# Float16 parts in the output product behind attention, and another order at attention's end

## The chip, the cores and the metric

One Trainium2 chip; the kernel runs on one NeuronCore of it. A core has five engines with a queue each: TensorE (PE, matrix products into PSUM; its weight loads, PEld, run beside it), VectorE (DVE), ScalarE (ACT), GpSimd (POOL) and SyncE (SP). SP and POOL issue most of the DMAs between HBM and SBUF. An engine works its queue in order and waits where an instruction's inputs or buffers are not ready. The metric is the device time of one execution in microseconds (us).

## The reference

A two-layer transformer block on 256 tokens of width 2048, with 256 context tokens beside them. Each layer normalises, shifts and scales its input by vectors made from the condition `c`, runs a mixer of width 4096 and multiplies the mixer's output by `w_out`, gated. Layer 0's mixer is a Fourier branch, for tokens and context. Layer 1's is attention: 64 query heads of size 64 share 8 key and value heads; a token sees a window of tokens and the whole context, with one sink per head. Cut to what matters here:

```python
q, k, v, z = split(h @ w_in)                 # layer 1
kc, vc = split(hc @ w_in[:, kv columns])
o = softmax([q k^T, sink]) v                 # keys: the window and the context
y = o * silu(z)                              # 256 x 4096
x = x + gate * (y @ w_out[1])                # 4096 x 2048: the product that is changed
return rmsnorm(x, final_g)
```

All inputs and the result are float32.

## The kernel before, in words

**Precision.** TensorE takes a product in parts: each operand is split into a high part and a remainder, and three matmuls (high x high, high x low, low x high) are summed in PSUM. `mm3` (lines 144 to 147) issues these three. There are two kinds of parts. With fp32r parts, `split` (lines 65 to 67) casts on ACT and subtracts on DVE, and nothing is scaled. With float16 parts, `split16` (lines 134 to 139) first multiplies by a power of two `up`, so that the parts fit float16's range; the result is scaled back where it leaves PSUM. The power of two comes from the sum of the squares of the whole tensor, so every weight that is to be split this way has to be read and squared once ahead of time.

**Layer 0's output product** (32 steps, lines 1031 to 1075) uses float16 parts in 28 of 32 contraction steps of each half. Beside it run: the squares of layer 1's key and value weights (`scan_loads1`, lines 812 to 822: POOL loads half a tile of 512 KB as two loads, `scan_sums` squares them on ACT, line 827), the adaptive vectors of layer 1 (line 792 on DVE, loads on SP and POOL; its `wa` buffers and the weight parts `wf` share the six buffers of the tag `ws`), and the squares of layer 0's output.

**The layer boundary** (lines 1078 to 1112) sums squares for the norm, turns the result x1 to rows and stores it to `x1d`.

**Keys and values** (lines 1137 to 1227). All 512 rows are split into float16 parts (`hz`, lines 1152 to 1156, on DVE and ACT), 16 contraction steps of 24 matmuls each against `wkv`, whose parts `split16` makes per half tile. In the same stage `make_hx1` (lines 1167 to 1173) builds the fp32r parts of the 256 tokens for the queries and gates.

**Attention** (lines 1234 to 1503). The work is laid out by hand as a list of filler units (`units`, queries, gates and, at the end, the first column block of the output product: 12 units `"o"` of two contraction steps each, 0 to 23) and 66 turns of a loop. Turn `i` emits the scores and the softmax of head `i` (`stage_s`), a filler unit, the product with the values of head `i - 2` (`stage_o`), and another unit. The weights of a head are cast to float16 parts `f` (ACT, DVE; lines 1439 and 1440) and transposed to `ft` by a DMA on SP (line 1442); the last two heads, 62 and 63, are instead transposed by TensorE and evacuated by ACT and DVE (`stage_t`, lines 1445 to 1450). `emit_y` multiplies head outputs with their gates into `y1`, two blocks of 128 channels per tile.

**The product behind attention** (lines 1506 to 1644). `y_split` (lines 1243 to 1249) makes fp32r parts of y: blocks 0 to 15 in the `h1` pool, 16 to 23 in `act` tiles, 24 to 31 in `ys` tiles of the last pool; the subtraction is GpSimd's up to block 23. The 2048 output columns are taken in three passes: `wo1a` (512 columns, in the units, the last four pairs of steps after attention), `wo1b` (1024 columns, 16 tiles of two steps) and `wo1c` (512 columns, 8 tiles of four steps). The weights are split by `half_split`, fp32r. `evac` multiplies by the gate `gbc`, adds x1 (read back from `x1d` into `x2`, eight POOL loads at the start) and squares for the last norm; `finish` scales and stores.

**Order.** The framework plans the order of each engine's queue when the program is built: a list by priority (program order) with a simulated time. `tc.issue_after(ins)` puts what is in its block behind `ins` on that instruction's engine; it is an order, not a wait.

Of the kernel before, what the change touches and what calls it, by code (L numbers as in the profile page):

```python
# [10 lines left out]
F32 = mybir.dt.float32  # L11
# [21 lines left out]
def tile_dit(ctx: ExitStack, tc: tile.TileContext, a: dict, out: bass.AP):  # L33
# [778 lines left out]
    scans1 = iter(range(16))  # L812

    def scan_loads1(n):
        for j in [next(scans1) for _ in range(n)]:
            for q in range(2):
                t = act()
                c = (j % 2 * 2 + q) * 512
                nc.gpsimd.dma_start(t, a["wkv"][j // 2][:, c : c + 512])
                c = j * 2 + q  # L820
                c += 80 if c < 28 else -28
                pend.append((t, scn[:, c : c + 1]))
# [34 lines left out]
    with tc.tile_pool(name="yp", reuse_waits="tile", bufs=32) as ypool:  # L857
# [142 lines left out]
        ada_rate = {**{i: 2 for i in (*range(6, 10), *range(17, 26))}, **{i: 0 for i in (14, 15, 16, 28, 29, 30, 31)}}  # L1000
        hbd = dram.tile([P, 2], F32, name="hbd")
# [26 lines left out]
        for i in range(32):  # L1028
# [9 lines left out]
            scan_loads1({14: 1, 15: 2, 16: 1, 26: 2, 27: 1}.get(i, 1) if 14 <= i < 28 else 0)  # L1038
# [38 lines left out]

    x1d = dram.tile([2, P, D], F32, name="x1d")
# [57 lines left out]
    with tc.tile_pool(name="h1", reuse_waits="tile", bufs=16) as h1p:  # L1136
# [4 lines left out]
        with tc.tile_pool(name="kvp", reuse_waits="tile", bufs=2) as kvp:  # L1141
# [24 lines left out]

            def make_hx1(k):
                hx = h1p.tile([P, 512], F32R, tag="h1", name="h1")
                t = kvp.tile([P, 512], F32, tag="ht", name="ht")[:, 0:N]
                V.scalar_tensor_tensor(t, x1[k][:, 0:N], gs1[:, k, 0:1], r_bc1[:, 0:N], op0=ALU.mult, op1=ALU.mult)  # L1170
                S.activation(hx[:, 0:N], t, AF.Identity, bias=sh1[:, k, 0:1])
                V.scalar_tensor_tensor(hx[:, N : 2 * N], t, sh1[:, k, 0:1], hx[:, 0:N].bitcast(F32), op0=ALU.add, op1=ALU.subtract)
                hx1.append(hx)

            o = [[psum() for _ in range(2)] for _ in range(4)]
            for kg in range(8):
                with tc.issue_after(ends[max(kg * 2 - 1, 0)][0] if kg else sq_end[0]), tc.issue_after(ends[max(kg * 2 - 1, 0)][1]):
                    if kg:
                        wr = raw(a["wkv"][kg])
                    w = [split16(wr, i, upk) if kg or i else w0 for i in range(2)]  # L1180
# [25 lines left out]

            l1 = psum()
# [23 lines left out]
        with tc.tile_pool(name="at", reuse_waits="tile", bufs=2) as at:  # L1231
# [11 lines left out]
            def y_split(k):  # L1243
                if 16 <= k < 24:
                    t = act(F32R)
                else:
                    t = (h1p if k < 16 else fin[0]).tile([P, 512], F32R, tag="h1" if k < 16 else "ys", name="ys", bufs=16)
                split(t[:, 0:N], t[:, N : 2 * N], y1[k // 2][:, (k % 2) * N : (k % 2 + 1) * N], GP if k < 24 else V)
                yh.append(t)

            def o1_step(k, os_, wh, wl):
                while len(yh) <= min(k + 4, NB - 1) and (len(yh) < 24 or fin):
                    y_split(len(yh))
# [60 lines left out]
            def units():  # L1314
# [15 lines left out]
                for k in range(12):  # L1330
                    yield "o", k, 0, None
# [69 lines left out]
            def emit_y(blk):  # L1401
# [5 lines left out]
                V.scalar_tensor_tensor(y1[blk // 2][:, (blk % 2) * N : (blk % 2 + 1) * N], obs[blk, 1], dsc[:, blk // 4 : blk // 4 + 1], szs.pop(blk), op0=ALU.mult, op1=ALU.mult)  # L1407

            def stage_s(i):
# [23 lines left out]
                for tb in range(2):  # L1433
                    if i < 62:
# [4 lines left out]
                    S.activation(f[:, 0:512], pt[tb], AF.Copy, scale=sm[:, tb : tb + 1])  # L1439
                    V.scalar_tensor_tensor(f[:, 512:1024], pt[tb], sm[:, tb : tb + 1], f[:, 0:512], op0=ALU.mult, op1=ALU.subtract)  # L1440
                    if i < 62:
# [47 lines left out]
            for i in range(66):  # L1489
# [3 lines left out]
                if i == 62:  # L1493
                    t = actp.tile([P, 1024], F16, tag="act", name="ident16")
                    ident16.append(t[:, 0:P])
                    S.copy(ident16[0], ident)
                if i < 64:
                    pts[i] = stage_s(i)
                if i - 2 >= 62:
# [7 lines left out]
        with tc.tile_pool(name="fin", reuse_waits="tile", bufs=1) as fp:  # L1507
# [3 lines left out]
            x2 = []  # L1511
            for tb in range(2):
                x2.append([act() for _ in range(4)])
                for c in range(4):
                    nc.gpsimd.dma_start(x2[tb][c], x1d[tb, :, c * 512 : (c + 1) * 512])
            fg = fp.tile([P, D], F32, name="fg")
# [16 lines left out]
            for k in range(24, NB, 2):  # L1533
                w = w1_next()
                for i in range(2):
                    o1_step(k + i, oA, *(t[:, i * 512 : (i + 1) * 512] for t in w))
            for tb in range(2):
                evac(tb, 0, oA[tb])
            o = [[psum() for _ in range(2)] for _ in range(2)]
            for kg in range(16):  # L1540
                w = ws_split(raw(a["wo1b"][kg]))
                for j in range(2):
                    k = kg * 2 + j
                    wh, wl = w[j]
                    for tb in range(2):
                        for c in range(2):
                            q = slice(c * 512, (c + 1) * 512)
                            mm3(o[tb][c], yh[k][:, tb * P : (tb + 1) * P], yh[k][:, N + tb * P : N + (tb + 1) * P], wh[:, q], wl[:, q], k == 0, k == NB - 1)
# [5 lines left out]
            def step(k, tb, wh, wl, q=slice(0, 512), first=0, last=NB - 1):  # L1554
                mm3(o[tb][:, q], yh[k][:, tb * P : (tb + 1) * P], yh[k][:, N + tb * P : N + (tb + 1) * P], wh[:, q], wl[:, q], k == first, k == last)
# [31 lines left out]
            for kg in range(8):  # L1587
                t = raw(a["wo1c"][kg])
                if kg < 5:
                    w = [(h[:, q], l[:, q]) for h, l in ws_split(t) for q in (slice(0, 512), slice(512, 1024))]  # L1590
                else:
                    w = []
                    for i in range(2):
                        if kg * 2 + i < 13:
                            for j in range(2):
                                h, l = act(F32R), act(F32R)
                                split(h, l, t[:, (i * 2 + j) * 512 : (i * 2 + j + 1) * 512])
                                w.append((h, l))
                        else:
                            h, l = half_split(t, i)  # L1600
# [121 lines left out]
```

## Time and profile before

| | |
|---|---|
| median of three runs | 1771.17 us (1769.23 to 1772.79) |
| profiled execution | 1773.51 us |
| its span, first to last instruction | 1771.7 us |
| granted TensorE clock, mean | 0.997 |
| HBM read | 400.43 MB |

How the stages lie in the profiled span, by the first and last instruction on their tiles:

| us | stage |
|---|---|
| 322 to 658 | layer 0's gates (float16 parts) |
| 658 to 998 | layer 0's output product |
| 998 to 1008 | layer boundary |
| 1008 to 1091 | keys and values |
| 1091 to 1618 | queries, gates, attention; first units of the last product from 1570 |
| 1618 to 1762 | the rest of the product behind attention |
| 1762 to 1772 | last norm and stores |

How to read the profile's rows. A group has its line, engine and operation, `out<-in` by the program's names, shapes and types, the count, then busy us in total and mean ns of one, then the idle time of the engine just before it and what ended that. A row of the timeline has the start, the length in us, engine, line, operation and names; in square brackets stands the idle time before it and who ended it. Matmuls overlap, so their lengths exceed the distance of their starts. A DMA group has the issuing queue, the count, the size of one and the median us from issue to landing.

### The profile page before, as it was taken

The numbers are of one execution on the slowest core, as the hardware profiler recorded it, in microseconds if no ns is written. First come the engines' busy times: TensorE is split into PE (matmuls) and PEld (weight loads), VectorE is DVE, ScalarE is ACT, GpSimd is POOL, SyncE is SP. The second block draws the span as 40 slices with busy tenths as digits, with TensorE's granted clock in tenths as the row PEclk, the third lists the DMA queues.
The fourth block names the chain that finished last, engine by engine and source line by source line (L and its number), as shares of the span: only waits on it lengthen the run. The fifth ranks groups of instructions, "written<-read, shape, count | busy, mean of one in ns | idle before, by whom it ended". The sixth has DMA issues, their size and how long they took to land. (4 is left out here: it accounts for less than half of the span.)

```text
span 1771.7 us, 26606 instructions
## 1 busy us (share of the span) xinstructions
PE 1733.6 (98%) x9517; PEld 1188.4 (67%) x9517; DVE 1405.9 (79%) x2454; ACT 1089.2 (61%) x2069; POOL 333.8 (19%) x440
## 2 busy tenths in 40 slices
PE   6999999999999999999999999999999999999997
PEld 4679999544444444446434745788888888887886
DVE  5778889697777786886688695899999999997455
ACT  5545556477777755464324454688888878886343
POOL 0002111212222114121201001412303230234010
PEclk9999999999999999999999999999999999999999
DMA  9998999778988869985976532688987898888544
GB/s 393 418 355 242 288 273 255 288 285 318 330 306 318 313 222 374 364 293 201 367 270 210 170 130 72 190 198 205 216 214 204 216 221 195 206 211 270 190 166 143
DMA packets 229077, 447.29 MB, mean 252 GB/s; under 512 B 155888, under 2 KB 156288, under 8 KB 202064
## 3 DMA queue, kind: packets, MB, share of 16 engines
q1 hardware_dynamic: 182784, 331.93, 58.0%
q0 software_dynamic: 42016, 106.70, 19.4%
q10 hardware_dynamic: 4144, 6.95, 1.2%
q8 instruction: 75, 1.23, 0.3%
q14 instruction: 58, 0.48, 0.1%
HBM read 400.43 MB, written 12.59 MB: 233 GB/s over the span
## 5 line engine op out<-in xcount | busy, mean ns | idle before, releaser
L67 DVE TENSOR_TENSOR wl<-raw,wh 128x1024 fp32r<-128x1024 f32 x197 | 262.6, 1338 | 111.1 <-ACT wh L66 83.0
L66 ACT CAST wh<-raw 128x1024 fp32r<-128x1024 f32 x197 | 205.5, 1045 | 145.5 <-PE ps L146 103.2
L146 PE MATMUL ps<-act,wf 128*128 128x512 f16 x512 | 194.2, 379 | 0.0
L147 PE MATMUL ps<-act,wf 128*128 128x512 f16 x512 | 191.3, 379 | 0.0
L145 PE MATMUL ps<-act,wf 128*128 128x512 f16 x512 | 189.9, 379 | 0.6 <-ACT wf L137 0.3
L1386 PE MATMUL ps<-h,wh 128*128 128x512 f32 x512 | 185.9, 399 | 0.0
L147 PEld LDWEIGHTS <-wf 128*128 128x128 f16 x960 | 93.9, 98 | 118.1 <-DVE wf L138 4.5
L145 PE MATMUL ps<-y,wf 128*128 128x512 f16 x448 | 170.6, 381 | 0.8 <-ACT wf L137 0.8
L147 PE MATMUL ps<-y,wf 128*128 128x512 f16 x448 | 167.3, 381 | 4.0 <-DVE wf L138 4.0
L146 PE MATMUL ps<-y,wf 128*128 128x512 f16 x448 | 170.7, 381 | 0.0
L145 PEld LDWEIGHTS <-wf 128*128 128x128 f16 x960 | 93.8, 98 | 113.6 <-ACT wf L137 4.2
L146 PEld LDWEIGHTS <-wf 128*128 128x128 f16 x960 | 94.0, 98 | 109.5 <-issue 0.8
L137 ACT ACTIVATE wf<-raw,nrm 128x1024 f16<-128x1024 f32 x56 | 63.2, 1145 | 137.8 <-PE ps L147 82.1
L1388 PE MATMUL ps<-h,wl 128*128 128x256 f32 x512 | 139.2, 282 | 0.0
L138 DVE SCALAR_TENSOR_TENSOR wf<-raw,tn,wf 128x1024 f16<-128x1024 f32 x64 | 79.8, 1282 | 42.5 <-ACT wf L137 42.4
L1440 DVE SCALAR_TENSOR_TENSOR f<-p,sm,f 128x512 f16<-128x512 f32 x128 | 104.6, 837 | 8.6 <-ACT f L1439 8.4
L1427 ACT ACTIVATE p<-ps,mx 128x512 f32<-128x512 f32 x128 | 87.8, 688 | 36.7 <-DVE mx L1424 31.8
L790 POOL DMA_DIRECT2D wa<-in_adw x64 | 34.0, 532 | 404.7 <-DVE acc L792 163.5
L1386 PEld LDWEIGHTS ps<-h,wh 128*128 128x128 f32 x512 | 96.9, 189 | 19.1
L1439 ACT ACTIVATE f<-p,sm 128x512 f16<-128x512 f32 x128 | 87.7, 717 | 30.8 <-DMA ft<-f 12.4
L146 PE MATMUL ps<-wl,h 128*128 128x512 f32 x256 | 101.3, 396 | 0.0
L827 ACT ACTIVATE act<-act 128x512 f32<-128x512 f32 x160 | 98.4, 616 | 4.7 <-DMA act<-in_wo 4.4
(414 smaller groups left out, 4676.4 us busy)
## 6 DMA issues: line engine op xcount, KB each, us to landing
raw<-in_wz SPq DMA_DIRECT2D x64, 1024.0 KB, 5.6
raw<-in_awp SPq DMA_DIRECT2D x32, 1024.0 KB, 12.7
zr<-in_adw SPq DMA_DIRECT2D x64, 512.0 KB, 6.9
wa<-in_adw POOLq DMA_DIRECT2D x64, 512.0 KB, 6.3
act<-in_wo POOLq DMA_DIRECT2D x128, 256.0 KB, 7.8
raw<-in_wo SPq DMA_DIRECT2D x32, 1024.0 KB, 8.0
raw<-in_wq SPq DMA_DIRECT2D x32, 1024.0 KB, 5.2
raw<-in_wu SPq DMA_DIRECT2D x32, 1016.0 KB, 6.3
```

The lines of the kernel that those rows point to most:

```text
L66: last_cast[0] = S.copy(h, src).ins
L67: last_sub[0] = eng.tensor_tensor(l, src, h.bitcast(F32), op=ALU.subtract).ins
L138: last_sub[0] = V.scalar_tensor_tensor(w[:, 1], src, up, w[:, 0], op0=ALU.mult, op1=ALU.subtract).ins
L145: PE.matmul(o, wh, xh, start=start, stop=False)
L146: PE.matmul(o, wh, xl, start=False, stop=False)
L147: return PE.matmul(o, wl, xh, start=False, stop=stop).ins
L827: S.activation(t, t, AF.Square, accum_out=c)
L1386: PE.matmul(o[0], wh[:, q], hx1[k], start=k == 0, stop=k == KT - 1)
L1388: PE.matmul(o[0][:, 0:N], wl[:, q], hx1[k][:, 0:N], start=False, stop=False)
L1427: S.activation(pt[tb], so[tb], AF.Exp, bias=mx[:, tb : tb + 1], scale=-1.0, accum_out=sm[:, tb : tb + 1])
L1439: S.activation(f[:, 0:512], pt[tb], AF.Copy, scale=sm[:, tb : tb + 1])
L1440: V.scalar_tensor_tensor(f[:, 512:1024], pt[tb], sm[:, tb : tb + 1], f[:, 0:512], op0=ALU.mult, op1=ALU.subtract)
```

## The change

The product behind attention takes float16 parts for contraction steps 0 to 27 in `wo1b` and `wo1c`; `wo1a`, which is worked on during attention, keeps fp32r parts, and so do steps 28 to 31.

- *Scales.* The sum of the squares of those weights (14 tiles of `wo1b` and 7 of `wo1c`, 42 half tiles) is added to the stream that squared the 16 half tiles of `wkv`. Seven of them are loaded in layer 0's product, with other counts per step (`w_rate`), and 35 in the keys' and values' stage (`loads2`, through four 512 KB buffers `pz`, on POOL), squared there by ACT or, one in three from the fourth weight tile on, by DVE (`sums2`). The squares of y are taken on ACT in attention (`y_sums`, one per tile of two blocks), and `out_scale` makes the powers of two at head 62.
- *Parts.* `y_half` makes float16 parts of y, two blocks at a time, in the `h1` pool, once attention's last cast has been issued, one tile per step. `split16` splits the weights. The weights of steps 28 to 31 are scaled too (`w_scaled`), and the gates' columns 512 and up are scaled back by `dn1`.
- *End of attention.* Head 61 is transposed by TensorE as 62 and 63 are. The list gets 14 units `"o"` (steps 0 to 27) instead of 12. All fp32r parts of y up to block 27 lie in the `h1` pool.
- *Order behind it.* The last two pairs of steps of `wo1a` and its evacuation (`first_rest`) come after the first two tiles of `wo1b`. Of the eight loads of `x2`, two stay at the start, and two each follow at tiles 3, 5 and 7.

```diff
-    scans1 = iter(range(16))
+    yq = adab[:, 1, 0].rearrange("p k s -> p (k s)")
+    wst = [a["wkv"][i] for i in range(8)] + [a["wo1b"][i] for i in range(14)] + [a["wo1c"][i] for i in range(7)]
+    scans1 = iter(range(58))
...
+        w_rate = {10: 1, 11: 1, 14: 2, 15: 2, 16: 2, 17: 1, 18: 1, 20: 1, 22: 1, 24: 1, 26: 2, 27: 2, 28: 3, 29: 2, 30: 1}
...
-            scan_loads1({14: 1, 15: 2, 16: 1, 26: 2, 27: 1}.get(i, 1) if 14 <= i < 28 else 0)
+            scan_loads1(w_rate.get(i, 0))
...
+    V.tensor_reduce(yq[:, 16:17], scn[:, 4:18], axis=AX.X, op=ALU.add)
...
+            def sums2(act_only):
+                for n in range(len(pend)):
+                    t, c = pend.pop(0)
+                    if n < 2 or act_only:
+                        S.activation(t, t, AF.Square, accum_out=c)
+                    else:
+                        V.tensor_tensor_reduce(t, t, t, 1.0, 0.0, ALU.mult, ALU.add, c)
+
+            def loads2(n):
+                for j in [next(scans1) for _ in range(n)]:
+                    t = kvp.tile([P, 1024], F32, tag="pz", name="pz", bufs=4)
+                    nc.gpsimd.dma_start(t, wst[j // 2][:, j % 2 * 1024 : j % 2 * 1024 + 1024])
+                    pend.append((t, scn[:, j - 23 : j - 22]))
...
-                    w = [split16(wr, i, upk) if kg or i else w0 for i in range(2)]
+                    w = []
+                    for i in range(2):
+                        w.append(split16(wr, i, upk) if kg or i else w0)
+                        with tc.issue_after(last_cast[0]), tc.issue_after(ends[min(kg * 4 + i * 2 + 1, 15)][0]):
+                            if kg * 2 + i < 12:
+                                sums2(kg < 3)
+                        with tc.issue_after(pow_end[0]):
+                            loads2((4, 3, 3, 3, 3, 3, 3, 3, 3, 3, 3, 1, 0, 0, 0, 0)[kg * 2 + i])
...
+            sums2(True)
+            V.tensor_reduce(yq[:, 17:18], scn, axis=AX.X, op=ALU.add)
...
-                if 16 <= k < 24:
-                    t = act(F32R)
-                else:
-                    t = (h1p if k < 16 else fin[0]).tile([P, 512], F32R, tag="h1" if k < 16 else "ys", name="ys", bufs=16)
+                t = (h1p if k < 28 else fin[0]).tile([P, 512], F32R, tag="h1" if k < 28 else "ys", name="ys", bufs=16 if k < 28 else 4)
...
+            def y_sums(n, i):
+                while ynext[0] < min(n, len(ypairs)) and ypairs[ynext[0]] <= i - 2:
+                    j = ynext[0]
+                    ynext[0] += 1
+                    S.activation(act(), y1[j], AF.Square, accum_out=yq[:, j : j + 1])
+
+            def out_scale():
+                V.tensor_reduce(yq[:, 18:19], yq[:, 0:14], axis=AX.X, op=ALU.add)
+                o = psum()
+                for c, i, st in ((0, 16, True), (0, 17, False), (1, 18, True)):
+                    PE.matmul(o[:, c : c + 1], ones.broadcast_to([P, P]), yq[:, i : i + 1], start=st, stop=i > 16)
...
+            def y_half(j):
+                t = h1p.tile([P, 1024], F16, tag="h1", name="yf", bufs=16)
+                S.activation(t[:, 0:512], y1[j], AF.Copy, scale=uy)
+                V.scalar_tensor_tensor(t[:, 512:1024], y1[j], uy, t[:, 0:512], op0=ALU.mult, op1=ALU.subtract)
+                for i in range(2):
+                    yf[j * 2 + i] = t[:, i * N : i * N + N], t[:, 512 + i * N : 512 + i * N + N]
...
+            def w_scaled(t, i):
+                h, l = (wsp.tile([P, 1024], F32R, tag="ws", name=n_) for n_ in ("wh", "wl"))
...
-                for k in range(12):
+                for k in range(14):
                     yield "o", k, 0, None
...
-                    if i < 62:
+                    if i < 61:
                         nc.sync.dma_start_transpose(ft[:, :, tb, :], f)
...
+                y_sums(14, i if i < 60 else 99)
+                if i == 62:
+                    out_scale()
...
-                if i - 2 >= 62:
+                if i - 2 >= 61:
                     stage_t(*pts[i - 2])
...
-            for k in range(24, NB, 2):
-                w = w1_next()
-                for i in range(2):
-                    o1_step(k + i, oA, *(t[:, i * 512 : (i + 1) * 512] for t in w))
-            for tb in range(2):
-                evac(tb, 0, oA[tb])
+            with tc.issue_after(f_last[0]), tc.issue_after(f_last[1]):
+                for j in range(3):
+                    y_half(j)
+
+            def first_rest():
+                for k in range(28, NB, 2):
+                    w = w1_next()
+                    for i in range(2):
+                        o1_step(k + i, oA, *(t[:, i * 512 : (i + 1) * 512] for t in w))
+                S.activation(gbc[:, 512:], gbc[:, 512:], AF.Copy, scale=dn1)
+                for tb in range(2):
+                    evac(tb, 0, oA[tb])
...
-                w = ws_split(raw(a["wo1b"][kg]))
+                if kg == 2:
+                    first_rest()
+                t = raw(a["wo1b"][kg])
+                with tc.issue_after(f_last[0]), tc.issue_after(f_last[1]):
+                    w = [split16(t, i, uw) if kg < 14 else w_scaled(t, i) for i in range(2)]
+                if kg + 3 < 14:
+                    with tc.issue_after(last_cast[0]), tc.issue_after(last_sub[0]):
+                        y_half(kg + 3)
+                if kg in (3, 5, 7):
+                    x2_load(kg // 2)
...
-                    w = [(h[:, q], l[:, q]) for h, l in ws_split(t) for q in (slice(0, 512), slice(512, 1024))]
+                    w = [(h[:, q], l[:, q]) for h, l in (split16(t, i, uw) for i in range(2)) for q in (slice(0, 512), slice(512, 1024))]
```

51 lines of the change are left out of this document (36 added, 15 removed).

## The prediction

> **What bounds the kernel now.** I read the page's busy times first, then the waits of TensorE, then a table by stretch, then the matmuls in order of time.
>
> ```profile
> span 1771.7 us, 26606 instructions
> PE 1733.6 (98%) x9517; PEld 1188.4 (67%) x9517; DVE 1405.9 (79%) x2454; ACT 1089.2 (61%) x2069; POOL 333.8 (19%) x440
> ```
>
> TensorE is busy 98% of the span: the time is the sum of its steps plus some 38 us in which it stands still.
>
> ```profile
> PE ps L145 <- DVE dh L254: 12.6, 2, 11.3
> PE ps L1457 <- DMA ft<-f: 4.4, 5, 2.1
> PE ps L147 <- DVE wf L138: 4.0, 1, 4.0
> ```
>
> (Total us, times, longest.) The first is the opening, which the change does not touch. The others lie where it works: five waits for transposes by DMA in attention, and one stall in layer 0's output product.
>
> ```profile
> 660.00:960.00 300.00, 295.18 (x1356) 141.07 (x1354) 232.42 (x358) 136.51 (x255) 66.09 (x124) 0.99 0.83 304
> 1008.00:1088.00 80.00, 80.00 (x373) 36.25 (x371) 60.09 (x116) 40.48 (x71) 0.00 (x0) 1.00 0.39 134
> 1160.00:1560.00 400.00, 399.00 (x2206) 332.83 (x2206) 375.10 (x698) 327.57 (x643) 85.35 (x60) 1.00 0.86 210
> 1590.00:1618.00 28.00, 25.70 (x151) 20.43 (x150) 23.08 (x45) 22.75 (x48) 14.01 (x18) 1.00 0.90 266
> 1628.00:1750.00 122.00, 122.00 (x528) 98.88 (x527) 67.92 (x62) 51.69 (x61) 11.83 (x6) 1.00 0.52 181
> ```
>
> A row has the stretch, its length, the busy time of PE, PEld, DVE, ACT and POOL, the granted clock, the DMA share and GB/s. The rows are layer 0's output product, the keys' and values' projection, attention, its end, and the product behind it. In the second and the last TensorE never stops: there only fewer or quicker matmuls shorten the time, and work added to ACT, DVE or DMA is free until TensorE waits for it.
>
> **The change part by part.** *Matmuls on float16 parts.* Durations overlap, so a matmul's price is the distance between starts. First layer 0's float16 product, then two stretches of the product that changes:
>
> ```profile
> 759.81 0.38 PE L145 MATMUL ps<-y,wf 128*128 128x512 f16 x1
> ...
> 767.58 0.38 PE L145 MATMUL ps<-y,wf 128*128 128x512 f16 x1
> ```
> ```profile
> 1640.00 1.10 PE L145 MATMUL ps<-wh,ys 128*128 128x512 f32 x4
> ...
> 1656.80 1.10 PE L145 MATMUL ps<-wh,ys 128*128 128x512 f32 x4
> ```
> ```profile
> 1676.32 1.07 PE L145 MATMUL ps<-wh,act 128*128 128x512 f32 x4
> ...
> 1689.92 1.07 PE L145 MATMUL ps<-wh,act 128*128 128x512 f32 x4
> ```
>
> Float16: 36 starts in 7.77 us, 215.8 ns. fp32r with y in ys tiles: six steps of 12 matmuls, 72 starts in 16.80 us, 233.3 ns. fp32r with y in act tiles (steps 16 to 23): 60 in 13.60 us, 226.7 ns. Of 32 steps 28 change, 20 of ys and 8 of act, each with 12 matmuls over wo1b and 6 over wo1c. That is 360 x 17.5 ns = 6.3 us and 144 x 10.9 ns = 1.6 us: **-7.9 us**, all of it on the path if the splits keep up.
>
> The Trainium skill (TensorE: Matmul & The Clock Gate, "Weight-path perf modes") says that the array takes one element per cell and cycle whatever its width; for 512 columns the page's start-to-start is 215.7 ns. By that fp32r would run at the same pace, and this term would be 0 instead of -7.9. The float16 rows agree to 0.1 ns; the fp32r rows are 17.6 ns off and decide.
>
> *The splits of that product.*
>
> ```profile
> L137 ACT ACTIVATE wf<-raw,adab 128x1024 f16<-128x1024 f32 x16 | 18.0, 1140 | 11.4 <-PE ps L146 4.4 <-PE ps L147 3.9 <-issue 2.4
> L138 DVE SCALAR_TENSOR_TENSOR wf<-raw,adab,wf 128x1024 f16<-128x1024 f32 x16 | 20.3, 1282 | 4.6 <-ACT wf L137 4.6
> L1439 ACT ACTIVATE f<-p,sm 128x512 f16<-128x512 f32 x128 | 87.7, 717 | 30.8 <-DMA ft<-f 12.4 <-issue 12.1 <-ACT th L1394 5.1
> L1440 DVE SCALAR_TENSOR_TENSOR f<-p,sm,f 128x512 f16<-128x512 f32 x128 | 104.6, 837 | 8.6 <-ACT f L1439 8.4
> ```
>
> A weight tile needs two halves and one y_half: ACT 2 x 1.14 + 0.72 = 3.0 us, DVE 2 x 1.28 + 0.84 = 3.4 us, against 24 x 215.8 ns = 5.2 us of matmuls. Covered, with 1.8 us to spare per tile. Scaling gbc, the three pairs of x2 loads moved down POOL's queue, and the last fp32r steps set behind two tiles have tens of us until their readers; on SP two wo1b tiles go ahead of the last wo1a tile, into three raw buffers as before. Taken at nothing; a cover that fails here costs at most one landing of a tile, some 5 us.
>
> *The end of attention.* Head 61 loses its two DMA transposes on SP and is turned by TensorE; 14 units of the first product instead of 12 fill the last slots, with four more y splits.
>
> ```profile
> 1600.80 0.27 PE L1457 MATMUL ps<-ft,v 128*128 128x256 f16 x1 [1.35 <-DMA ft<-f]
> ...
> 1601.67 0.83 PE L1449 MATMUL ps<-ident,f 128*128 128x128 f16 x12
> ...
> 1612.10 0.28 PE L1457 MATMUL ps<-ft,v 128*128 128x256 f16 x1 [0.94 <-DVE ft L1450]
> ```
>
> The first stall is head 61's: 1.35 us go. The second lies where slots were empty; 24 matmuls now stand there: up to 0.94 us go. 16 more transposes at 0.83 / 12 = 0.07 us are +1.1. out_scale puts three one-column matmuls into TensorE's queue, behind a VectorE sum of squares that are ready by head 60: +0.2 by the same row; the units queued behind them on TensorE would wait with them, if the squares were late. Two more evacuations on busy ACT and DVE, and y_half 0 to 2 with the first split between head 63's last cast and the product's first matmul: ACT 3 x 0.72 + 1.14, DVE 3 x 0.84 + 1.28, some 4 us while 24 to 30 matmuls of 0.23 us, 6 to 7 us, are still queued. What is late next is head 62's own evacuation. I take -0.5; bounds -2.3 (the stalls go, the rest hides) and +4 (nothing of those 4 us hides).
>
> *Squares of y*: 14 on ACT in attention. An existing square with its accumulator read follows its neighbour at 0.61 us:
>
> ```profile
> 894.70 0.61 ACT L827 ACTIVATE act<-act 128x512 f32<-128x512 f32 x1
> ...
> 895.31 0.61 ACT L827 ACTIVATE act<-act 128x512 f32<-128x512 f32 x1
> ```
>
> 14 x 0.61 = 8.6 us, against 400 - 327.6 = 72 us of idle ACT in the attention row. They queue ahead of exponentials and casts, but every head has two turns of slack. +0.5, bounds 0 and +4.
>
> *Squares of the output weights in layer 0's product*: 7 more half tiles, 14 loads and 14 squares, 8.6 us of an ACT that idles 163 of 300 us, and 3.7 MB.
>
> ```profile
> 921.49 1.23 DVE L792 CUSTOM_DVE_ANT_0 wa<-wa,cb 128x1024 f32<-128x1024 f32 x1 [3.27 <-DMA wa<-in_adw]
> ```
> ```profile
> 920.00:925.00 5.00, 1.02 (x4) 0.46 (x5) 3.51 (x6) 2.24 (x5) 0.00 (x0) 0.95 0.77 306
> 925.00:930.00 5.00, 5.00 (x18) 1.92 (x17) 5.00 (x10) 1.18 (x3) 0.53 (x1) 0.71 0.54 169
> ```
>
> The 4 us stall is this ring: VectorE waits for a wa load, the ws buffer it holds keeps ACT from the next wf split, TensorE runs dry, and the clock comes back at 0.71 for 5 us, another 1.5. The Trainium skill (the same page, Part 1) has the clock halve after an idle window of some 3.4 us; this gap was longer than that, and the trace agrees. The new rates thin the loads of these steps (5 half tiles in steps 17 to 25 instead of 9), but the surplus must land somewhere in this stage. 0, bounds -6 (the stall goes) and +6 (a second one).
>
> *Squares in the keys' and values' stage.* 35 half tiles of 512 KB through four pz buffers, loads on POOL, which is idle there.
>
> ```profile
> L645 ACT ACTIVATE pz<-pz 128x1024 f32<-128x1024 f32 x12 | 12.7, 1062 | 2.6 <-DMA pz<-in_wz 2.6
> ```
> ```profile
> wa<-in_adw POOLq DMA_DIRECT2D x64, 512.0 KB, 6.3
> ```
> ```profile
> act<-in_wkv POOLq DMA_DIRECT2D x32, 256.0 KB, 11.3
> ```
> ```profile
> 1039.32 1.15 ACT L137 ACTIVATE wf<-raw,adab 128x1024 f16<-128x1024 f32 x1
> ```
>
> 29 squares go to ACT: 40.5 + 29 x 1.06 = 71 of 80 us. 6 go to DVE, at some 1.3 us each: 60.1 + 8 = 68. Both fit, barely. The danger is the ring: a buffer takes issue, landing and square, about 0.5 + 6.3 + 1.1 = 7.9 us, so a load every 2.0 us, and the 31 behind the first four take 61 us. The steps that hold them last 11 x 24 x 215.8 ns = 57 us. 4 us late, ACT's split behind a square with it; but the split for step 11 was made at 1039, and its matmuls start 57 us after 1008: 26 us ahead. So nothing is lost until the landing passes about 9 us; from there each further us costs 31 / 4 = 7.8. The hz and hx1 casts, on the same queue, come later too. I take +1.5, nearer the row of the same 512 KB than the 256 KB one; bounds 0 and, at 11.3 us, +18.
>
> Sum: -7.9 - 0.5 + 0.5 + 0 + 1.5 = **-6.4 us**. The profiled execution took 1773.5 (span 1771.7 and 1.8 around it), so 1767.1; it lies 2.3 above the median of the runs shown, 1771.17, which gives **1765**.
>
> **The rivals.** *Two stalls go*: the ring at 920 clears with the thinner loads, -5.5 more: 1759 to 1757. For it: the loads leave just those steps; against it: the doubled wa traffic stays. *The ring of pz buffers binds*: the slower one. Demand in this stage is 8 tiles of 1 MB and 35 of 0.5, 26 MB in 80 us, 330 GB/s, more than the 304 of layer 0's row, whose 256 KB loads took 11.3 us. If the landing passes 9 us ACT's queue stands behind squares, TensorE waits for splits, and the clock falls as at 925. At 11.3 us: 1765 + 17 = 1782; slower from 10.3 us on. Against it: queue orders are planned, and squares seldom waited before. *No quicker pace*: fp32r and float16 alike here, only the side costs left, 1771.2 + 1.5 = 1773. Against it: the rows above. *Many small costs*: the upper ends at attention's end, its squares and the 920 ring, each about half, eat the gain: 1768 to 1775.
>
> **How the numbers follow.** Forecast 0.58, with a range of its own of 1760 to 1767.6; two stalls 0.12; pz ring 0.12; no quicker pace 0.05; small costs 0.13. A measurement tells 0.2% from nothing, 3.5 us: faster is below 1767.6, slower above 1774.7. Faster 0.58 + 0.12 = 0.70; same 0.05 + 0.11 = 0.16; slower 0.12 + 0.02 = 0.14. The range 1756 to 1774 leaves out the ring and a little at either end.
>
> **What would show it.** Right: starts at 215.8 ns over wo1b and wo1c, and a stretch from the product's first to its last matmul about 8 us shorter; no wait for transposes by DMA at head 61; TensorE full between the keys' first and last matmul, and that stage still 83 us. Wrong: waits of TensorE for splits there, with ACT waiting for pz loads; a second stall beside 920; TensorE idle between head 63 and the first float16 matmul.

## The result, and the profile after

| | before | after |
|---|---|---|
| median | 1771.46 us (12 runs, 1766.05 to 1774.63) | 1771.95 us (12 runs, 1770.11 to 1774.54) |
| profiled execution, its span | 1773.51, 1771.7 us | 1770.58, 1768.8 us |
| HBM read | 400.43 MB | 422.45 MB |

The recorded ratio to the kernel before, which is not simply the quotient of the two medians, is 0.9998, with a 95% interval of 0.9988 to 1.0009: no change that can be told from none. The time lies in the range of 1756 to 1774, but the forecast of 1765 was 7 us too low, and the most likely outcome, faster, did not come. That the time still lies in the range is luck: without a gain of 2.8 us in layer 0 that the prediction had taken at nothing (e2 below), it would be 1774.8.

The page's busy times after the change:

```profile
span 1768.8 us, 26913 instructions
PE 1728.3 (98%) x9539; PEld 1143.4 (65%) x9539; DVE 1426.8 (81%) x2489; ACT 1151.0 (65%) x2199; POOL 362.2 (20%) x489
```

TensorE's busy time fell by 5.3 us and the span by 2.9, so in all it stands still 2.4 us longer than before. The waits of TensorE say where (total us, times, longest):

```profile
PE ps L145 <- DVE dh L254: 12.9, 2, 11.6
PE ps L1238 <- ACT act L1225: 4.9, 1, 4.9
PE ps L1524 <- DMA ft<-f: 3.0, 4, 2.0
PE ps L146 <- DVE wl L67: 2.2, 3, 1.6
...
PE ps L997 <- DVE act L991: 1.6, 1, 1.6
```

Before, the second and the last two were absent or 0.2 us; the 4.0 us of layer 0's stall (L147 waiting for `wf`) are gone. The same stretches as in the prediction, moved with the stages, with layer 0's 860 to 960 beside them (length, busy PE, PEld, DVE, ACT, POOL, granted clock, DMA share, GB/s):

```profile
660.00:960.00 300.00, 299.24 (x1383) 143.55 (x1382) 236.97 (x365) 144.24 (x275) 70.30 (x133) 1.00 0.85 314
1004.00:1084.00 80.00, 80.00 (x372) 36.27 (x371) 64.55 (x121) 65.85 (x120) 16.37 (x31) 1.00 0.94 343
1160.00:1560.00 400.00, 397.81 (x2186) 329.71 (x2185) 371.40 (x695) 332.48 (x666) 86.70 (x60) 1.00 0.86 208
1590.00:1628.00 38.00, 36.41 (x214) 28.96 (x213) 36.10 (x64) 32.12 (x55) 9.36 (x14) 1.00 0.96 305
1640.00:1750.00 110.00, 110.00 (x505) 55.55 (x504) 73.21 (x67) 57.18 (x67) 12.54 (x6) 1.00 0.53 182
860.00:960.00 100.00, 100.00 (x465) 45.39 (x464) 89.72 (x144) 39.36 (x66) 11.21 (x22) 1.00 0.81 290
```

Layer 0's product no longer stops in 860 to 960. The keys' and values' stage is still full, with ACT up from 51% to 82% busy and the DMA share up from 0.39 to 0.94. So no cost shows in the stage where the squares stand. It shows right behind it. The timeline there (start, us; in brackets what the engine had waited for):

```profile
1088.13 1.06 ACT L1177 ACTIVATE pz<-pz 128x1024 f32<-128x1024 f32 x1 [2.82 <-DMA pz<-in_wo1c]
...
1089.31 0.19 DVE L1235 TENSOR_REDUCE adab<-scn 128x1 f32<-128x35 f32 x1 [2.00 <-ACT pz L1177]
...
1090.12 0.57 ACT L1224 COPY act<-ps 128x512 f32<-128x512 f32 x1
...
1090.60 0.60 ACT L1225 ACTIVATE act<-ps 128x512 fp32r<-128x512 f32 x1
...
1091.25 0.80 PE L1238 MATMUL ps<-act,oner 128*128 128x512 f32 x1 [4.89 <-ACT act L1225]
```

The stage's last matmul starts at 1085.98. The copies that empty its PSUM banks (L1224, L1225) stand in ACT's queue behind the last square, whose half tile lands at 1088.1, and a weight cast of 1.0 us behind that; VectorE stands behind the sum of the 35 results, which waits for the same square. In the program's text the last square and the sum come after the copies; the planned order put them ahead. TensorE is out of work for 4.9 us, and gets half its clock up to 1095.6:

```profile
1085.00:1090.00 5.00, 1.36 (x7) 0.39 (x4) 1.92 (x4) 2.18 (x5) 0.00 (x0) 0.88 0.73 288
1090.00:1095.00 5.00, 3.75 (x9) 2.98 (x10) 4.45 (x9) 5.00 (x11) 0.00 (x0) 0.50 0.00 0
```

The product behind attention did what was forecast. Thirty starts of its float16 matmuls:

```profile
1645.13 0.38 PE L145 MATMUL ps<-wf,yf 128*128 128x512 f16 x1
...
1651.60 0.38 PE L145 MATMUL ps<-wf,yf 128*128 128x512 f16 x1
```

6.47 us, 215.7 ns each, and in the row of 1640 to 1750 above TensorE never waits. The stretch from the last scores to the end is 9.5 us shorter (next table); it holds the same number of matmuls on the weights before and after.

From the starts of seven matmuls that mark the stages, the lengths of the stages are as follows, in us, for all kernels of this study. The marks are: first and last matmul on `y` in layer 0; first and last on `hz`; the first product of a head with its values; the last score matmul of head 63; the last matmul. A last column gives the median.

| kernel | layer 0's product | boundary | keys, values | to the first head | attention | end | median |
|---|---|---|---|---|---|---|---|
| before | 318.7 | 31.2 | 82.7 | 54.4 | 454.0 | 163.3 | 1771.4 |
| after | 312.7 | 32.6 | 82.7 | 61.5 | 458.5 | 153.8 | 1771.95 |
| no squares in the keys' stage (e1) | 312.8 | 31.2 | 82.7 | 54.3 | 462.1 | 153.8 | 1764.39 |
| layer 0 alone (e2) | 312.8 | 31.2 | 82.7 | 54.3 | 452.3 | 166.0 | 1768.64 |
| product alone (e3) | 318.3 | 31.2 | 82.7 | 54.3 | 454.8 | 155.0 | 1762.79 |
| last squares later (e4) | 312.8 | 31.2 | 82.7 | 54.8 | 458.2 | 153.8 | 1763.71 |
| no squares of y (e5) | 312.8 | 31.2 | 82.7 | 63.2 | 453.6 | 153.8 | 1767.66 |
| e4 with the sink moved (e6) | 312.8 | 31.2 | 82.7 | 54.8 | 456.8 | 153.8 | 1761.24 |
| e4 without squares of y (e7) | 312.8 | 31.2 | 82.7 | 54.8 | 456.0 | 153.8 | 1760.20 |
| e6 with squares of y on GpSimd (e8) | 312.7 | 31.2 | 82.7 | 54.9 | 472.1 | 153.8 | 1776.14 |
| last square behind the copies (e9) | 312.8 | 31.2 | 82.7 | 57.4 | 459.7 | 153.8 | 1766.32 |

The lengths are of one profiled execution each. Before layer 0's product, and in the code that no kernel touches, these executions differ by up to 3.1 us (its first matmul starts between 657.9 and 661.0), so a sum over one row does not give that kernel's median. Differences in us below are differences of medians; the intervals are some 2 to 3 us either way.

### The profile page after: what moved, and what is told of

It is laid out like the page before. It is cut to its first block, busy times and chain, and to the rows that moved or that the text cites. A ratio compares the mean times of both kernels' runs of the same rounds, so it can differ in the third digit from the quotient of the medians.

```text
span 1768.8 us, 26913 instructions
## 1 busy us (share of the span) xinstructions
PE 1728.3 (98%) x9539; PEld 1143.4 (65%) x9539; DVE 1426.8 (81%) x2489; ACT 1151.0 (65%) x2199; POOL 362.2 (20%) x489
## 3 DMA queue, kind: packets, MB, share of 16 engines
q8 instruction: 75, 1.23, 0.3%
HBM read 422.45 MB, written 12.59 MB: 246 GB/s over the span
## 5 line engine op out<-in xcount | busy, mean ns | idle before, releaser
L67 DVE TENSOR_TENSOR wl<-raw,wh 128x1024 fp32r<-128x1024 f32 x152 | 201.4, 1326 | 40.3 <-ACT wh L66 37.3
L146 PE MATMUL ps<-act,wf 128*128 128x512 f16 x512 | 194.0, 379 | 0.0
L147 PE MATMUL ps<-act,wf 128*128 128x512 f16 x512 | 191.1, 379 | 0.0
L66 ACT CAST wh<-raw 128x1024 fp32r<-128x1024 f32 x152 | 158.2, 1041 | 27.6 <-PE ps L146 18.8
L146 PE MATMUL ps<-y,wf 128*128 128x512 f16 x448 | 169.8, 379 | 0.0
L147 PEld LDWEIGHTS <-wf 128*128 128x128 f16 x960 | 93.8, 98 | 113.2
L147 PE MATMUL ps<-y,wf 128*128 128x512 f16 x448 | 166.5, 379 | 0.0
L146 PEld LDWEIGHTS <-wf 128*128 128x128 f16 x960 | 93.9, 98 | 109.1
L1453 PE MATMUL ps<-h,wl 128*128 128x256 f32 x512 | 138.7, 281 | 0.3 <-DVE wl L67 0.3
L829 ACT ACTIVATE act<-act 128x512 f32<-128x512 f32 x174 | 107.1, 616 | 20.2 <-DMA act<-in_wo1b 13.5
L146 PE MATMUL ps<-wl,h 128*128 128x512 f32 x256 | 102.5, 401 | 0.5 <-DVE wl L67 0.4
```

The costliest lines, as they stand in the source:

```text
L66: last_cast[0] = S.copy(h, src).ins
L67: last_sub[0] = eng.tensor_tensor(l, src, h.bitcast(F32), op=ALU.subtract).ins
L146: PE.matmul(o, wh, xl, start=False, stop=False)
L147: return PE.matmul(o, wl, xh, start=False, stop=stop).ins
L829: S.activation(t, t, AF.Square, accum_out=c)
L1453: PE.matmul(o[0][:, 0:N], wl[:, q], hx1[k][:, 0:N], start=False, stop=False)
```

## The experiments

My first theory, from the two traces: three things eat the gain. They are the squares in the keys' and values' stage, which hold up the copies behind them; the squares of y in attention; and, smaller, a wait at the layer boundary. The rivals: the new product is itself worth less than its matmuls, or the longer attention is only another order of the queues.

**e1: the keys' and values' stage without the squares.**

```diff
-                            loads2((4, 3, 3, 3, 3, 3, 3, 3, 3, 3, 3, 1, 0, 0, 0, 0)[kg * 2 + i])
+                            pass
```

(and `scn` set to a constant)

> The changed kernel without the 35 half tiles loaded and squared in the keys' and values' stage; their sum is a constant (0.25 per column). Theory A (squares whose loads land late stand ahead of that stage's evacuation on ACT and DVE): no wait of the sum over the values for ACT, which cost 4.9 us there, and no half clock behind it, some 2 us more: 7 us faster than the changed kernel, so about 1764 to 1765, 0.4% below the kernel before. Rival B (the gain was lost elsewhere, in attention or at its end): the same time as before, within 0.2%.

Measured: 1764.39 us (6 runs), ratio 0.9961, 0.9946 to 0.9976. That is 7.6 us less than after, and the stretch from the last `hz` matmul to the first product of a head is back at 54.3 us. The 18 MB of reads (404.10 MB in all here, 422.45 after) and 35 squares were covered as long as the stage's matmuls ran; the cost stands behind them, and it is nearly what the product gains. The attention of 462 us belongs to the one profiled execution: at 1767.04 us it is the longest of the six, with 7.3 us of waits for transposes by DMA.

**e2: the change in layer 0 alone.** The kernel before, with the new list of loads in layer 0's product and 23 half tiles in place of 16.

```diff
-            scan_loads1({14: 1, 15: 2, 16: 1, 26: 2, 27: 1}.get(i, 1) if 14 <= i < 28 else 0)
+            scan_loads1(w_rate.get(i, 0))
```

> The kernel before with only the changed stream of squares in layer 0's output product: 23 half tiles at the new rates instead of 16; the sum over the 7 more is made and not used. Theory A (the new rates removed the 4 us stall of the wf split in that stage): no such stall, about 5 to 6 us faster than before, 1766. Rival B (the stall comes and goes by itself): a stall of 4 us there again or none, and a median within 2 us of before. Rival C (7 more half tiles cost something): slower than before by 1 to 5 us.

Measured: 1768.64 us (12 runs), ratio 0.9985, 0.9974 to 0.9997. The stall at 920 is gone here too, and with it 5.9 us of layer 0's product, but only 2.8 us of the median. In this profile 2.7 us come back at the end of attention (166.0 for 163.3), where an evacuation of transposed weights comes 1.7 us late and the granted clock is at half from 1607.7 to 1611.1 behind it; whether every execution loses them, one profile does not tell.

**e3: the product alone.** The change without any of its new squares, and with the old loads in layer 0; the three sums are constants.

```diff
-                y_sums(14, i if i < 60 else 99)
...
+                GP.memset(yq[:, 18:19], 17025179.0)
```

> The changed kernel without any square that the float16 product needs: old rates and 16 half tiles in layer 0, none in the keys' stage, none of y; the sums are constants of the right size. It is the product, head 61's turn and the new order alone. Theory A (the product gains what its matmuls' pace gives, and attention's end 1 us): 8 to 10 us faster than before, 1762 to 1763, with the stall of layer 0 as before. Rival B (the product gains less because its start or its splits hold it): less than 5 us faster.

Measured: 1762.79 us (6 runs), ratio 0.9946, 0.9929 to 0.9963: 8.6 us faster than before. With the old loads the stall in layer 0 is there again:

```profile
PE ps L147 <- DVE wf L138: 3.7, 1, 3.7
```

Old loads, two profiles, two stalls, of 4.0 and 3.7 us; new loads, nine profiles, none. So the spacing of the loads makes the stall, not chance. Together e2 and e3 give 1771.4 - 2.8 - 8.6 = 1760.0 us, which is what the change would be worth if its other squares were free.

**e4: the last eight half tiles later.** All the work is done; 27 half tiles stay in the keys' and values' stage, the last eight are loaded and squared beside the first query units, in `act` tiles of half that size.

```diff
-                            loads2((4, 3, 3, 3, 3, 3, 3, 3, 3, 3, 3, 1, 0, 0, 0, 0)[kg * 2 + i])
+                            loads2((4, 3, 3, 3, 3, 3, 3, 3, 2, 0, 0, 0, 0, 0, 0, 0)[kg * 2 + i])
...
+                if i < 8:
+                    late_loads()
```

> The changed kernel, but 27 half tiles in the keys' and values' stage (none loaded after its ninth half tile of weights) and the last 8 behind it, beside the first query units, in act tiles. Theory A: the evacuation behind the last key matmuls no longer stands behind late squares, so the 4.9 us wait and the half clock go, at most 1 to 2 us come back from ACT's work beside the first queries: 5 to 7 us faster than the changed kernel, 1765 to 1767. Rival B (the ring of loads is late from the start, and the hz and split work is what is late): the wait stays at 3 us or more and the time within 2 us of the changed kernel.

Measured: 1763.71 us (6 runs), ratio 0.9955, 0.9939 to 0.9971. Faster than both kernels, and not to be told from e1, which squares none of the 35 half tiles. The two stretches in this kernel's trace:

```profile
1015.00:1080.00 65.00, 65.00 (x303) 29.46 (x301) 53.20 (x101) 53.41 (x98) 11.07 (x21) 1.00 0.87 319
1085.00:1090.00 5.00, 5.00 (x24) 3.13 (x23) 3.67 (x6) 4.53 (x9) 0.00 (x0) 1.00 0.00 0
```

ACT is 82% busy and the loads run at 319 GB/s, nearly as after the change, but the last square is over when the copies are due, and TensorE goes on without a gap at full clock.

That left 1764.39 - 1760.0 = 4.4 us, which e1 has and the sum of e2 and e3 has not. The candidates were the squares of y, and the planner, which lays all queues of attention anew whenever something in them changes.

**e5: no squares of y.** The changed kernel without them; **e7: e4 without them.** The edit is that of e3's first line and last constant.

> The changed kernel with the 14 squares of y in attention left out; the sum that they make is set to a constant, so the scale of the output product is not computed from y. Everything else stays. Theory: what the first four runs left over is the price of these squares. The product alone gave 1762.79 - 1771.39 = -8.6 us, layer 0 alone -2.8; together 1760.0, and the version without squares in the keys' and values' stage, which has both and the squares of y, took 1764.39, 4.4 more. So this kernel takes 1771.9 - 4.4 = 1767.5, and attention from its first product of heads to the last scores is 454 to 455 us as in the product-only run, not 458.5. Rival: the longer attention comes with any other order of the queues and the squares are free: 1771 to 1772, and attention stays at 458.

> The version with the last eight half tiles of squares moved behind the keys' and values' stage, and the squares of y left out as in the run before (a constant for their sum). If the prices add up, it takes 1763.7 - 4.4 = 1759.3 us, about what the product alone and layer 0 alone give together (1760.0). If the squares of y are free, 1763.7.

Measured: e5 1767.66 us (12 runs), ratio 0.9979, 0.9968 to 0.9991; e7 1760.20 us (6 runs), ratio 0.9932, 0.9918 to 0.9946. Expected were 1767.5 and 1759.3. The squares of y cost 4.3 us in the one kernel and 3.5 in the other. The pair e4 and e7 is the cleaner one: in e5's profile the gap behind the keys' stage is 7.1 us, against 4.9 in after, which makes its stretch to the first head 63.2 us, and e4 and e7 have no such gap. The stretch of attention from the first product of a head to the last scores, in after and in e5:

```profile
1147.44:1605.94 458.50, 454.47 (x2489) 376.00 (x2490) 427.68 (x796) 382.81 (x778) 121.32 (x93) 1.00 0.85 207
```

```profile
1147.96:1601.59 453.63, 452.47 (x2489) 376.37 (x2490) 428.64 (x793) 375.00 (x750) 119.59 (x93) 1.00 0.85 210
```

TensorE stands still for 4.0 us with the squares and 1.2 without; ACT is 83.5% busy and 82.7%. So it is not that ACT fills up. In after, TensorE waits 2.5 us there for `wl` parts (L146 and L1453, four waits), in e5 0.8 (one). VectorE makes `wl` from ACT's cast, but no square holds up these casts: in all four waits the cast had been over for 0.8 us or more when its subtraction began, and VectorE had worked without a pause for at least 6 us before that. The longest comes 25 us after the last square of y, which starts at 1568.7:

```profile
1588.10 1.04 ACT L66 CAST wh<-raw 128x1024 fp32r<-128x1024 f32 x1
...
1589.28 2.43 DVE L1507 SCALAR_TENSOR_TENSOR f<-p,sm,f 128x512 f16<-128x512 f32 x2
...
1592.52 1.21 DVE L67 TENSOR_TENSOR wl<-raw,wh 128x1024 fp32r<-128x1024 f32 x1
...
1593.78 0.50 PE L146 MATMUL ps<-wl,ys 128*128 128x512 f32 x1 [1.58 <-DVE wl L67]
```

The part is late in VectorE's queue, behind two subtractions of head weights and another step. This wait of 1.6 us is in the profiles of all kernels that square y on ACT (after, e1, e4, e6, e9) and not in e5 and e7, where one of 0.7 to 0.8 us stands, nor in e3. Waits for transposes are 1.0 and 0.4 us, and 2.0 us of the difference lie in TensorE's busy time and were not followed. These parts are from one profile each; the 3.5 to 4.3 us are from medians. So the cost goes with the squares; whether their time on ACT makes it, or the other order of VectorE's queue that the plan has with them, was not told apart.

**e6: the sink's steps moved.** In after, VectorE waits at the layer boundary for a small load whose landing took 6.2 us there and 4.2 before:

```profile
987.21 0.19 DVE L1126 TENSOR_SCALAR nsink<-sink 128x64 f32<-128x64 f32 x1 [1.28 <-DMA sink<-in_sink]
```

e6 is e4 with this step and its neighbour moved behind the keys' and values' stage.

> The version with the last eight half tiles moved, and VectorE's two small steps on the attention sink moved from the boundary between the layers to the end of the keys' and values' stage, so that nothing at the boundary waits for the sink's load. Nothing is left out. Theory: the 1.3 us for which VectorE waited there in the changed kernel came from one landing of 6.2 us; in the version with later squares it landed in 4.5 and nobody waited, so this changes nothing: 1763 to 1764. Rival: most executions have the wait, and this takes 1.4 us off: 1762.3.

Measured: 1761.24 us (6 runs), ratio 0.9946, 0.9929 to 0.9963. Its interval overlaps that of e4, and the boundary takes 31.2 us in the profiles of both, so it isn't shown that the move helps; the 1.4 us of the boundary appear in after's profile alone. e6 has the lowest median of the kernels here that do the whole work: 10.1 us below before.

**e8: the squares of y on GpSimd.** e6 with GpSimd multiplying, folding 512 columns to 16 and adding up.

```diff
-                    S.activation(act(), y1[j], AF.Square, accum_out=yq[:, j : j + 1])
+                    t = act()
+                    GP.tensor_tensor(t, y1[j], y1[j], op=ALU.mult)
+                    for c in (256, 128, 64, 32, 16):
+                        GP.tensor_tensor(t[:, 0:c], t[:, 0:c], t[:, c : 2 * c], op=ALU.add)
```

> The kernel of the run before, with the squares of y made by GpSimd instead of ScalarE: a product, five additions that fold 512 columns to 16, and one that adds them up, for each of 14 tiles. Nothing is left out. A GpSimd operation on 128x256 takes 1.08 us here, so a tile takes some 2.2 + 1.1 + 0.5 + 0.3 + 0.2 + 0.1 + 0.1 = 4.5 us, 63 us in all of the 330 that GpSimd idles in attention. If ScalarE's time is the price of these squares, the time falls by up to 4.4: 1759 to 1760. Rival: GpSimd's queue also splits y and issues loads, and these come late behind 4.5 us of work: 1764 or more.

Measured: 1776.14 us (11 runs), ratio 1.0026, 1.0015 to 1.0037, 15 us worse than e6. The rival, 1764 us or more, is what came, and 12 us more than that. The last tile's chain on GpSimd, and who waits for it:

```profile
1571.33 1.04 POOL L1286 TENSOR_TENSOR act<-act 128x512 f32<-128x512 f32 x1 [0.36 <-DVE act L1481]
...
1585.13 1.32 POOL L1288 TENSOR_TENSOR act<-act 128x64 f32<-128x64 f32 x1
...
1590.29 1.23 POOL L1288 TENSOR_TENSOR act<-act 128x32 f32<-128x32 f32 x1
...
1594.43 0.22 POOL L1292 TENSOR_TENSOR adab<-adab,act 128x16 f32<-128x16 f32 x1
```

```profile
DVE adab L1295 <- POOL adab L1292: 3.3, 1, 3.3
```

```profile
1597.83 0.79 PE L146 MATMUL ps<-wl,ys 128*128 128x512 f32 x1 [3.30 <-DVE wl L67]
```

The seven steps are spread over 23 us between the splits of y in the same queue; VectorE's sum (L1295) waits 3.3 us for the last, the next `wl` part behind it on VectorE comes late, and TensorE stops for 3.3 us. That is one of several such places. From the first product of a head to 1620 us TensorE waits 14.0 us in e8 and 5.8 in e6, and the granted clock is at half for 3.4 us three times in e8's attention (from 1140.0, 1440.4 and 1597.4), in e6's never. By an estimate from these, 8.2 us more of waits and 4.5 us for the clock (1.5 each, as worked out in the last section), that is most of the 15.3 us by which attention is longer.

**e9: order or traffic.** The changed kernel with all loads and squares in place; only the very last square, and VectorE's sum, go behind the copies.

```diff
-            sums2(True)
-            V.tensor_reduce(yq[:, 17:18], scn, axis=AX.X, op=ALU.add)
+            with tc.issue_after(ev):
+                sums2(True)
...
+            V.tensor_reduce(yq[:, 17:18], scn, axis=AX.X, op=ALU.add)
```

(`ev` is the last copy on ACT; the sum follows the loop over the values)

> The changed kernel with all its work and all its loads; only the last square of a pz buffer on ScalarE and VectorE's sum over the 35 results are set behind the copies that empty the keys' and values' PSUM banks, instead of ahead of them. Theory: TensorE's gap there is a matter of order in the queues alone. ScalarE's copies stood behind a square whose data landed at 1088.1, VectorE's rotations behind a sum that waited for that square; with both moved the copies start when the last matmul ends, the stretch from the stage's last matmul to the first product of a head falls from 61.5 us to 54.4 to 54.9, and the time from 1771.9 by some 7 to 1765, with the same traffic. Rival: the 340 to 350 GB/s of the loads make the weights or the copies late, whatever the order: the stretch stays over 60 us and the time at 1770 to 1772.

Measured: 1766.32 us (12 runs), ratio 0.9966, 0.9953 to 0.9979: 5.6 us less than after with the same bytes moved, and the stretch to the first head falls from 61.5 to 57.4 us. So most of the cost is order, not traffic; the figures forecast were 1765 and 54.4 to 54.9. What is left of the gap:

```profile
PE ps L145 <- DVE rt L1137: 2.5, 1, 2.5
```

```profile
1084.19 0.58 ACT L1224 COPY act<-ps 128x512 f32<-128x512 f32 x1
...
1085.68 1.23 DVE L1179 CUSTOM_DVE_ANT_0 pz<-pz 128x1024 f32<-128x1024 f32 x1 [3.68 <-DMA pz<-in_wo1c]
...
1086.84 0.69 DVE L1132 TENSOR_TENSOR act<-ps,act 128x512 f32<-128x512 f32 x1
...
1089.37 1.06 ACT L1177 ACTIVATE pz<-pz 128x1024 f32<-128x1024 f32 x1
```

ACT's copies now start on time, but VectorE has a late square of its own (L1179), and the rotations of the keys (L1132, L1137) stand behind it. It is the same fault on the other engine, which I had not moved.

## Why the prediction missed the outcome: which of its steps held and which failed

In medians the terms add up: -8.6 (product and end of attention, e3), -2.8 (layer 0, e2), +4.3 (squares of y, after less e5), +7.6 (squares in the keys' stage, after less e1) are +0.5; after less before is +0.49. With some 2 to 3 us of uncertainty in each term, so close a match is luck; that no large term is missing is what it shows.

- **Matmuls on float16 parts, -7.9, and the splits, 0: right.** The starts are 215.7 ns apart, TensorE never waits in 1640 to 1750, and the end stage is 9.5 us shorter in eight of the nine profiles with the new product, and 8.3 in e3's. The Trainium skill's rule (TensorE: Matmul & The Clock Gate, "Weight-path perf modes"), which the page states beside fp8 and bf16 and by which fp32r would go at float16's pace, would have put this gain at 0; the trace and e3's median decide against it for fp32r.
- **End of attention, -0.5: right in sign.** Of the 9.5 us some 1.6 are left for it; the wait at head 61 is gone, and nothing stands between head 63's last matmul at 1628.38 and the first float16 matmul at 1628.49.
- **Layer 0, 0 with -6 to +6: the low side came.** I left the stall at its place because the wa traffic stays. It goes with the new spacing of the loads each time: 5.9 us of that stage, 2.8 (0.5 to 4.6) of the median.
- **Squares of y, +0.5 with 0 to +4: the upper end came**, 3.5 to 4.3. The failing step is "every head has two turns of slack": it looks at the heads alone. With the squares, parts of the filler units' weights come late in VectorE's queue, 2.5 us of waits for 0.8 (e5); by what way the squares on ACT bring that about stays open.
- **Squares in the keys' and values' stage, +1.5: the step that failed most**, 7.6. The sentence was "nothing is lost until the landing passes about 9 us". The medians of the landings were near what I took:

```profile
pz<-in_wo1b POOLq DMA_DIRECT2D x21, 512.0 KB, 7.2
...
pz<-in_wo1c POOLq DMA_DIRECT2D x14, 512.0 KB, 6.4
```

A load went out every 2.36 us (34 steps from 1000.8 to 1081.1), not every 2.0: four buffers make a round of 9.4 us, against my 7.9. The landings are one part: they are 7.4 us in the mean (3.9 to 13.1; the first eight 7.8 to 13.1), not 6.3. The other is that a landed tile waits for its turn in ACT's or VectorE's queue, 0.8 us in the mean, which I had left out. By my 61 us the last load would have gone out some 17 us before 1081. I asked whether the splits would be late, found 26 us of lead, which was right, and stopped there. I did not ask what comes next in the two queues when the stage ends: the copies. The price there is the gap of 4.9 us and, with the clock at 0.50, some 2 us more: nine matmuls at 0.42 us, from 1091.84 to 1095.65, for 0.23.
- **The rivals.** The ring's rival named the right place and wanted a landing of over 10 us for it; it came at 7, over another waiter. "Many small costs" had the time right, 1768 to 1775, but by other costs: of its three, only the squares of y came, and the largest, in the keys' stage, was not among them. "Two stalls go" came as well and is hidden by the costs. I had taken these as alternatives, where parts of three happened together.

## What to carry to other kernels

When work is put into idle time of an in-order queue, follow its last piece to the end of the stage and ask what stands behind it there; a lead of 26 us for the stage's own inputs says nothing about its outputs. The time of a ring is issue, landing, waiting for a turn, and use, so a round taken without the waiting is a lower bound. A filler that costs nothing on the busy share (ACT at 82.7% without it and 83.5% with it here) can still come with 4 us of cost; look at the queues of the other engines for it, too.

## What the runs showed of the hardware

- What a gap does to the clock depends on where it falls, not on its length alone. In these traces the granted clock is at half for stretches of 3.41 us, or of 6.83 us, in and behind the gaps of 4.9 us in after and 7.1 us in e5. Gaps of 2.5 us go either way: e4's (1139.92 to 1142.41) has half clock behind it, e6's at the same place (1138.02 to 1140.50) and e9's (1085.82 to 1088.33) have not. I cut each trace into cells of 3.41 us that begin where its half-clock stretches begin. The cell that holds most of the gap, and the next one, in e4, e6 and e9 (the third figure from the right is the granted clock):

```profile
1139.62:1143.03 3.41, 0.93 (x8) 0.59 (x7) 2.12 (x5) 3.27 (x7) 2.67 (x2) 1.00 0.98 183
1143.03:1146.44 3.41, 3.41 (x12) 2.74 (x11) 3.41 (x7) 1.77 (x5) 3.41 (x4) 0.50 1.01 316
```

```profile
1138.88:1142.29 3.41, 1.79 (x12) 1.58 (x13) 3.00 (x3) 2.78 (x6) 3.41 (x3) 1.00 1.01 256
1142.29:1145.70 3.41, 3.41 (x21) 2.99 (x20) 3.38 (x8) 1.95 (x6) 3.41 (x4) 1.00 1.03 253
```

```profile
1086.74:1090.15 3.41, 1.82 (x8) 1.53 (x9) 3.38 (x10) 3.39 (x6) 0.00 (x0) 1.00 0.49 208
1090.15:1093.56 3.41, 3.41 (x17) 2.73 (x16) 1.86 (x3) 1.36 (x3) 0.00 (x0) 1.00 0.02 5
```

TensorE is busy for 27% of e4's cell, but for 52% and 53% of the others, whose gaps lie across two cells. In all eleven traces, from 25 to 1750 us, every cell with TensorE busy for 42% or less has half clock behind it (17 cells), and no cell with 51% or more has. The kernel before loses its clock this way after a gap of 2.07 us, from 1146.4 to 1149.8. The Trainium skill (TensorE: Matmul & The Clock Gate, Part 1) puts the idle window that halves the clock at some 3.4 us; the length of the stretches agrees with it, but here gaps of 2 to 2.5 us were enough where they fell into one cell. So e9's full clock behind its gap is luck of the moment; where the clock does halve, the same gap costs some 1.5 us more (an estimate: 3.4 us at 0.42 us a matmul in place of 0.23).

- GpSimd's time for an addition does not follow its size in e8: 1.23 us on 128x32 at 1590.29, which ends within 0.2 us of a VectorE subtraction of 128x1024 (1589.65 to 1591.41) that itself took 1.76 us, and 0.22 us on 128x16 when VectorE was elsewhere. That the two engines hinder each other is the likely reading; no run here tests it by itself.
- The keys' stage took 343 GB/s for 80 us at a DMA share of 0.94, and its loads of 512 KB landed in 6.4 to 7.2 us (medians). In layer 0's product, at a share of 0.85 and 314 GB/s, most of the loads of half that size took longer, those of `wkv`, and the rest, for `wo1b`, as long:

```profile
act<-in_wkv POOLq DMA_DIRECT2D x32, 256.0 KB, 10.7
...
act<-in_wo1b POOLq DMA_DIRECT2D x14, 256.0 KB, 7.0
```

I had taken the busier DMA for the slower landing; by these rows neither the share nor the size sets it alone. What does was not tried.
